# The last four pairs of gate column tiles as seven block products in place of two full ones

## The chip, the cores and the metric

The kernel is one launch on one core of one Trainium2 chip. The metric is the device time of that launch in microseconds (us), taken as the median of several runs; a lower time is better. The engines are named as the profile names them: PE (TensorE, matrix products), PEld (its weight loads), DVE (VectorE), ACT (ScalarE), POOL (GpSimd) and SP (SyncE, which here only issues DMA transfers). Each engine works through its own list of instructions in order and waits on semaphores that other engines and DMA transfers raise.

## The reference, cut to what matters

One decoder layer over 512 tokens of width 1024, all in float32:

```python
proj = h @ w_in                       # 1024 columns in, 4096 out
q, k, v, p, g = split(proj, [512, 1024, 1536, 2048])   # g: 2 x 1024 gate logits
y_attn = moba_attention(q, k, v, rel_bias) @ w_branch_attn
y_pool = multiscale_pool(p, w_pool_group, pool_scale) @ w_branch_pool
gates  = sigmoid(g).reshape(B, S, 2, D)
mixed  = gates[:, :, 0] * y_attn + gates[:, :, 1] * y_pool
h = layer_norm(ALPHA * h + mixed @ w_out, ln1_g, ln1_b)
a, u = split(h @ w_ffn_in, 2)         # 1024 columns in, 2 x 2816 out
f = (gelu(causal_dwconv(a, conv_w, conv_b)) * u) @ w_ffn_out
h = layer_norm(ALPHA * h + f, ln2_g, ln2_b)
```

The change concerns the 2 x 1024 gate columns `g`. Gate tile (0, f) is columns 128 f to 128 f + 127 of the attention gate, (1, f) the same columns of the pool gate; the two with one f are a column pair. The code numbers them `("g", f)` and `("g", 8 + f)`.

## The kernel before, in words

**Precision.** Every large product is made of three products of float32r parts: a tile is split into `hi` (a rounded copy, made on ACT) and `lo` (the rest, made on DVE); `split`, lines 65 to 70. `mm3` (lines 182 to 186) then issues hi·hi, hi·lo and lo·hi.

**Weights.** All weight tiles stand in one list, `chunks`, in the order of their use. `weights(i)` (line 177) fetches ahead up to chunk i + LEAD (3): a transfer issued on SP into one of three `wraw` buffers, then the split into one of RING (5) slots of `whi` and `wlo`.

**Stages.** (1) x is loaded and split into `xT_hi`, `xT_lo` (8 row tiles of 128 x 512, the first named dimension being the contraction). (2) v. (3) Attention in four pairs of heads; `bg()` (line 425) places one column tile of q, k, p or g (24 matmuls of 512 columns, `in_tile`, line 341) between the steps of a head: `scores`, `trans`, `pv`. At head pair 3 the steps and tiles are: scores 6, tile, scores 7, tile, `trans(6)`, tile, `trans(7)`, tile, `pv(3)`. (4) The gate tiles left in `todo` follow without a break: the gates of the first twelve tiles are copied to `gates` by DVE and put through the sigmoid later in place, the last four (NLATE) go through the sigmoid straight into `late`. Meanwhile zT (pool branch) and oT (attention) are split (lines 456 to 459). (5) The branch products `br`, the output projection `wo`, LayerNorm, (6) the channel mixer `fi`, in which ten column pairs (SEVEN, line 40) are made by seven block products, and (7) `fo` with the final LayerNorm.

**Seven block products** (`seven`, lines 693 to 717, for the channel mixer). A column pair has weights A and U of 1024 x 128 each; the 1024 rows are cut in halves k1, k2 and the 512 tokens in halves t1, t2, so that the pair is a 2 x 2 by 2 x 2 block product. Two full tiles need 2 x 24 = 48 matmuls of 512 columns; the seven products need 7 x 12 = 84 of 256 columns. They need, on the activation side, four differences of blocks (T3, nT1, nT2, T4, made by `t_form`, line 663, each 128 x 1024 and each split), and on the weight side, besides A and the second half D of U, two sums: X = U + shifted A, brought by a plain transfer on SP and a second one on POOL that adds as it lands (`fetch_sums`, line 126), and Y, made by two DVE additions (line 144). Three PSUM banks (sa, sb, sc) are taken for a pair; ACT copies three partial sums out (lines 699, 701, 705) and DVE adds three (708, 710, 711). The last product of a pair is held back (`pending`) and issued in the middle of what follows.

**What sets the order.** The program is written in one sequence, and a scheduler that has its own estimate of times places the instructions in the lists of the engines. Tile pools hand out memory; a pool with `reuse_waits="tile"` makes a new tile wait only for the users of the memory that it takes over.

## Time and profile before

| | |
|---|---|
| runs of the kernel before | 651.28, 652.33, 652.54 us, median 652.33 us |
| the profiled execution, its own time | 652.89 us |
| its span, first to last instruction | 651.2 us |
| time outside the span (launch and end) | 652.89 - 651.2 = 1.7 us |
| DVE, ACT, POOL busy | 432.7, 318.1, 106.9 us |
| granted TensorE clock, mean | 0.996 |

How to read the rows in the next part: a timeline row is start, duration (both us), engine, source line, operation, output<-inputs, shapes, count, and in brackets the idle time of that engine ahead of it and what ended it. Rows of groups give busy time and the mean duration of one in ns. A matmul's duration reaches into the next ones; the distance between the starts of two matmuls is what one costs while PE is full. A row with x4 covers four instructions from the start of the first to the end of the last.

### The profile page before, as it was taken

What the parts mean: (1) busy time and instruction counts of PE and PEld (TensorE: products, weight loads), DVE (VectorE), ACT (ScalarE), POOL (GpSimd) and SP (SyncE); (2) the same over time, 40 slices, a digit from 0 to 9 for tenths busy, and PEclk for the clock granted to TensorE, in tenths of its full rate; (3) what the DMA queues carried; (4) which work ended last, traced back from release to release, by engine and by line L of the source; (5) the groups of instructions that cost most, each with busy time, mean ns of one, the idle gap of its engine ahead of it and who ended that gap; (6) DMA issues with size and microseconds to landing.
All of it is one profiled execution on the core that took longest, in us unless ns stands there. A gap on an engine that the chain in (4) does not pass through costs nothing.

```text
span 651.2 us, 8945 instructions
## 1 busy us (share of the span) xinstructions
PE 639.8 (98%) x3442; PEld 548.0 (84%) x3442; DVE 432.7 (66%) x638; ACT 318.1 (49%) x455; POOL 106.9 (16%) x149
## 2 busy tenths in 40 slices
PE   9999999999999999999999999999999999999994
PEld 6888787878788888889999999989898888888884
DVE  6456665564632576299677766776866859798596
ACT  6547556675522333225544544445455337555352
POOL 1605261211000123300010000101000202123302
PEclk9999999999999999999999999999999999999998
DMA  9633222222222237404066665556335895899905
GB/s 324 229 124 104 82 81 82 67 67 94 72 94 100 90 98 285 135 1 161 2 164 171 167 158 160 153 156 165 101 98 162 289 254 131 215 200 201 261 3 129
DMA packets 30363, 91.63 MB, mean 141 GB/s; under 512 B 3560, under 2 KB 3816, under 8 KB 30064
## 3 DMA queue, kind: packets, MB, share of 16 engines
q1 hardware_dynamic: 21744, 65.86, 30.3%
q0 software_dynamic: 8000, 24.14, 18.4%
q10 hardware_dynamic: 576, 1.05, 0.4%
q8 instruction: 27, 0.44, 0.3%
q14 instruction: 16, 0.13, 0.1%
HBM read 87.87 MB, written 3.17 MB: 140 GB/s over the span
## 4 chain that ended last, share of the span: by engine, by line
PE 91%; DVE 3%; DMA 2%; ACT 1%; POOL 1%; issue 1%; DVEq 0%; ACTq 0%; POOLq 0%
PE fi L184 7%; PE fi L186 7%; PE fi L185 7%; PE g L184 5%; PE g L186 4%; PE g L185 4%; PE v L285 3%; PE sa L186 3%; PE sa L184 3%; PE sa L185 3%; PE wo L186 2%; PE br L186 2%; PE wo L185 2%; PE br L185 2%; PE wo L184 2%; PE br L184 2%
## 5 line engine op out<-in xcount | busy, mean ns | idle before, releaser
L70 DVE TENSOR_TENSOR wlo<-wraw,whi 128x1024 fp32r<-128x1024 f32 (+1 forms) x115 | 141.4, 1232 | 69.9 <-ACT whi L69 68.6
L69 ACT ACTIVATE whi<-wraw 128x1024 fp32r<-128x1024 f32 (+1 forms) x114 | 114.6, 1009 | 129.7 <-PE g L185 23.7
L186 PE MATMUL fi<-hT_hi,wlo 128*128 128x512 f32 (+1 forms) x232 | 81.8, 353 | 0.0
L185 PE MATMUL fi<-hT_lo,whi 128*128 128x512 f32 (+1 forms) x232 | 81.8, 353 | 0.0
L184 PE MATMUL fi<-hT_hi,whi 128*128 128x512 f32 (+1 forms) x232 | 81.5, 354 | 0.0
L184 PE MATMUL g<-xT_hi,whi 128*128 128x512 f32 x128 | 50.3, 393 | 0.0
L186 PE MATMUL g<-xT_hi,wlo 128*128 128x512 f32 x128 | 49.9, 390 | 0.0
L185 PE MATMUL g<-xT_lo,whi 128*128 128x512 f32 x128 | 49.9, 390 | 0.0
L186 PEld LDWEIGHTS fi<-hT_hi,wlo 128*128 128x128 f32 x232 | 43.9, 189 | 5.8
L185 PEld LDWEIGHTS fi<-hT_lo,whi 128*128 128x128 f32 x232 | 43.9, 189 | 5.6
L184 PEld LDWEIGHTS fi<-hT_hi,whi 128*128 128x128 f32 x232 | 43.6, 189 | 5.4
L132 POOL DMA_DIRECT2D xraw<-in_w_fi x10 | 12.2, 1220 | 176.2 <-DMA xraw<-in_w_fi 91.9
L69 ACT ACTIVATE whi<-tw 128x1024 fp32r<-128x1024 f32 (+1 forms) x30 | 29.3, 982 | 21.7 <-DMA tw<-in_w_fo 8.5
L70 DVE TENSOR_TENSOR wlo<-tw,whi 128x1024 fp32r<-128x1024 f32 (+1 forms) x30 | 33.3, 1126 | 7.5 <-ACT whi L69 7.5
L186 PEld LDWEIGHTS g<-xT_hi,wlo 128*128 128x128 f32 x128 | 24.0, 188 | 5.1
L184 PEld LDWEIGHTS g<-xT_hi,whi 128*128 128x128 f32 x128 | 24.0, 188 | 5.0 <-issue 0.2
L185 PEld LDWEIGHTS g<-xT_lo,whi 128*128 128x128 f32 x128 | 24.0, 188 | 4.9
L390 POOL TENSOR_SCALAR pp<-pp,rs 128x128 f32<-128x128 f32 (+3 forms) x32 | 21.7, 695 | 37.5 <-PE g L186 18.4
L482 POOL TENSOR_TENSOR mt<-m,m 128x512 f32<-128x512 f32 x8 | 11.1, 1393 | 96.0 <-DVE m L479 79.3
L172 POOL DMA_DIRECT2D tw<-in_w_fo x18 | 15.6, 897 | 60.6 <-DVE wlo L70 60.6
L184 PE MATMUL wo<-whi,mx_hi 128*128 128x512 f32 x64 | 25.0, 391 | 0.0
L186 PE MATMUL wo<-whi,mx_lo 128*128 128x512 f32 x64 | 24.9, 390 | 0.0
(250 smaller groups left out, 1665.0 us busy)
## 6 DMA issues: line engine op xcount, KB each, us to landing
wraw<-in_w_fi SPq DMA_DIRECT2D x34, 512.0 KB, 4.3
wraw<-in_w_c SPq DMA_DIRECT2D x28, 512.0 KB, 3.4
tw<-in_w_fo POOLq DMA_DIRECT2D x20, 512.0 KB, 8.0
xraw<-in_w_fi SPq DMA_DIRECT2D x10, 512.0 KB, 4.4
xraw<-in_w_fi POOLq DMA_DIRECT2D x10, 512.0 KB, 5.8
wraw<-in_w_fo SPq DMA_DIRECT2D x10, 512.0 KB, 5.8
tw<-in_w_fo SPq DMA_DIRECT2D x10, 512.0 KB, 6.4
wraw<-in_w_br SPq DMA_DIRECT2D x8, 512.0 KB, 3.3
```

The costliest lines, as they stand in the source:

```text
L69: nc.scalar.activation(hi, src, AF.Copy)
L70: nc.vector.tensor_tensor(lo, src, hi.bitcast(F32), op=ALU.subtract)
L132: nc.gpsimd.dma_start(v, bass.AP(tensor=a.tensor, offset=a.offset, ap=[[pst, pn], [u.offset + S - a.offset, 2], [est, S]]), accum_op=ALU.add)
L172: nc.gpsimd.dma_start(raw, half(then[1:], sl), accum_op=ALU.add)
L184: nc.tensor.matmul(out_, wh, ah, start=start, stop=False, **kw)
L185: nc.tensor.matmul(out_, wh, al, start=False, stop=False, **kw)
L186: nc.tensor.matmul(out_, wl, ah, start=False, stop=stop, **kw)
L285: nc.tensor.matmul(bs[j], xs_[j][a], (wh, wl)[b], start=kt == 0 and n == 0, stop=False)
L390: nc.gpsimd.tensor_scalar(pp[:, offs[i]:offs[i] + n], pp[:, offs[i]:offs[i] + n], rs[:, i:i + 1], 1.0, op0=ALU.mult, op1=ALU.mult)
L482: nc.gpsimd.tensor_tensor(mt, m[1], m[0], op=ALU.add)
```

## The change

- The order of the column tiles gets "s" entries: after q, k, p and the gate tiles (0,0), (1,0), (0,1), (1,1) come (0,2), (1,2), (0,3), then the pairs f = 4 to 7 as seven products each, and (1,3) last. `bg()` stops at the first "s" entry, so that (0,3) is the last plain tile before `pv(3)`.
- `seven`, `s_mm`, `fetch_seven`, `fetch_sums` and `t_form` become general: the same code serves gates and channel mixer.
- After `pv(3)` a pool `gx` is opened on the memory of the attention tiles. Four transfers on POOL bring x again as four quarters (`quad0` to `quad3`, each 128 x 4 x 256, 512 KB), two more per pair bring X. Then the four differences are formed and split, then the pairs run.
- A pair's gates leave through ACT: `gates_done` applies the sigmoid to bank sa and to u (with scale -1).
- The splits of zT and oT now stand behind the gate pairs, ahead of `br`.

The core of the diff:

```diff
-    order += spare
+    order += [("g", 2), ("g", 10), ("g", 3)] + [("s", f) for f in range(4, KT)] + [("g", 11)]
...
     def in_tile(n):
         kind, j = order[n]
-        wh, wl = split3(weights(C0 + n), KT)
+        if kind == "s":
+            seven(("g", j), (xT_hi, xT_lo), tg, p1s[j % 2], gus[j % 2],
+                  lambda ba, u, j=j: gates_done(j, ba, u))
+            return
+        wh, wl = split3(weights(at[kind, j]), KT)
...
+    def gates_done(j, ba, u):
+        nc.scalar.activation(new_gate(j), ba, AF.Sigmoid)
+        nc.scalar.activation(new_gate(KT + j), u, AF.Sigmoid, scale=-1.0)
...
-    bg(len(todo))
     attn.close()
+    late = actp.enter_context(tc.tile_pool(name="late", bufs=1, side="right", reuse_waits="tile")).tile(
+        [P, NLATE, S], F32, name="late")
+    gxs = ExitStack()
+    gx = gxs.enter_context(tc.tile_pool(name="gx", bufs=1, reuse_waits="tile"))
...
+    quads = []
+    for k in (k1, k2):
+        for t in (t1, t2):
+            v = gx.tile([P, 4, 256], F32, name=f"quad{len(quads)}")
+            nc.gpsimd.dma_start(v, xT[k.start * P:k.stop * P, t].rearrange("(k p) t -> p k t", p=P))
+            quads.append(v)
+    fetch_sums(sums.pop(0))
+    for n in ("nT1", "T3", "nT2", "T4"):
+        t_form(n, tg, *quads)
+    while todo:
+        in_tile(todo.pop(0))
+    flush()
+    gxs.close()
...
-    while todo:
-        in_tile(todo.pop(0))
```

The general pieces that it calls (the first product to the last, in the order written):

```python
def t_form(n, tt, b11, b12, b21, b22):
    if n in ("nT1", "T3"):
        v, a = {"nT1": (b11, b11), "T3": (b12, b22)}[n]
        nc.vector.tensor_tensor(v, a, b12, op=ALU.subtract)
    else:
        v, a = {"nT2": (b22, b11), "T4": (b21, b22)}[n]
        nc.vector.scalar_tensor_tensor(v, a, -1.0, v, op0=ALU.mult, op1=ALU.subtract)
    split(*tt[n], v)

# seven(key, whole, tt, y, u, done):
s_mm(key, "A", 0, b_(k1, t1), chain, True);   nc.scalar.activation(y, chain, AF.Copy)
s_mm(key, "X", 0, tt["T3"], low, True);       nc.scalar.activation(u[:, t2], low, AF.Copy)
flush()
s_mm(key, "Y", 0, tt["nT2"], chain, False);   nc.scalar.activation(u[:, t1], chain, AF.Copy)
s_mm(key, "A", 1, b_(k2, t1), c11, True)
s_mm(key, "D", 0, tt["T4"], low, False);      nc.vector.tensor_tensor(u[:, t1], u[:, t1], low, op=ALU.add)
s_mm(key, "X", 1, tt["nT1"], chain, False);   nc.vector.tensor_tensor(u[:, t2], u[:, t2], chain, op=ALU.add)
nc.vector.tensor_tensor(ba[:, t1], y, c11, op=ALU.add)
# held back: s_mm(key, "Y", 1, b_(k2, t2), chain, False); done(ba, u)
```

In the program as built, the lists of the engines run as follows from the last softmax on. The index in brackets is the pair, "A0" the first half product with weights A, and so on; the lists are the scheduler's.

```
PE    g(0,3) | pv(3) | A0[4] x12 | X0[4] x1 | A1[4] x12 | Y0[4] x1 | A0[5] x2 | X0[4] x11 | X0[5] x2, A1[5] x2,
      Y0[4] x1, D0[4] x1, Y0[4] x10, A0[5] x10, A1[5] x10, X1[4] x12, X0[5] x6, D0[4] x11, ... (pairs interleaved)
      ... Y0[7] x10 | g(1,3) x23 | X1[7] x12 | g(1,3) x1 | Y1[7] x12 | br(0) ...
ACT   sigmoids | copy oT of pv(3) | copy y of A0[4] | nT1_hi | whi X[4] | whi D[4] | T3_hi | nT2_hi | whi Y[4] |
      whi A[5] | whi X[5] | T4_hi | copies u[4] | ...
DVE   copy of g(0,3) | nT1 | nT1_lo | T3 | first half of Y[4] | nT2 | second half of Y[4] | wlo X[4] | wlo D[4] | T4 |
      T3_lo | nT2_lo | wlo Y[4] | wlo A[5] | wlo X[5] | T4_lo | ...
      ... add u[7] behind X1[7] | wlo br(2) | add y + c11 into bank sa[7] | wlo br(3) | zT_lo x4 | oT_lo x4 | ...
POOL  softmax scaling of head 7 x4 | quad0 | quad1 | quad2 | quad3 | adding transfer X[4] | adding transfer X[5] | ...
SP    X[4] | X[5] (both behind the last scores) | A[5] (behind the second half of Y[4], whose input it overwrites) | ...
```

quad0 waits for the last matmul of scores 7. The matmul X0[4] x1 needs T3_hi and whi X[4]; the first of Y0[4] needs nT2_hi and whi Y[4]; the first of A0[5] needs whi A[5]; the first of X0[4] x11 needs T3_lo; the first of Y1[7] waits for the addition into bank sa[7]. The channel mixer and all that follows keep their lists.

## The prediction, on record before the run

> **What bounds the kernel now.** I read the page first: shares of the engines, then the chain that ended last; then the timeline of PE where the change sits, then the rows that price what is added.

> ```profile
> span 651.2 us, 8945 instructions
> PE 639.8 (98%) x3442; PEld 548.0 (84%) x3442; DVE 432.7 (66%) x638; ACT 318.1 (49%) x455; POOL 106.9 (16%) x149
> PE 91%; DVE 3%; DMA 2%; ACT 1%; POOL 1%; issue 1%; DVEq 0%; ACTq 0%; POOLq 0%
> ```

> PE is busy for 98% of the span and holds 91% of the chain. So a matmul less is time won, and a wait of PE is time lost in full. The stretch with the gate tiles shows no gap at all, while DVE and ACT have half of it free:

> ```profile
> 165.00:185.00 20.00, 20.00 (x89) 16.53 (x89) 10.47 (x14) 8.99 (x14) 0.00 (x0) 1.00 0.29 92
> ```

> (columns: PE, PEld, DVE, ACT, POOL busy us, granted clock, DMA share, GB/s). That is an average over 20 us. The change puts four differences and their splits at one point of it, so the point decides, not the average.

> **What is removed from PE.** Eight gate tiles (192 matmuls of 512 columns) become 336 of 256 columns.

> ```profile
> 164.25 0.50 PE L184 MATMUL g<-xT_hi,whi 128*128 128x512 f32 x1
> ...
> 173.90 0.39 PE L184 MATMUL g<-xT_hi,whi 128*128 128x512 f32 x1
> ...
> 179.34 0.39 PE L184 MATMUL g<-xT_hi,whi 128*128 128x512 f32 x1
> ...
> 349.01 0.28 PE L184 MATMUL sa<-hT_hi,whi 128*128 128x256 f32 x1
> ...
> 350.44 0.28 PE L184 MATMUL sb<-T_hi,whi 128*128 128x256 f32 x1
> ```

> From 173.90 to 179.34 lie 24 matmuls of 512 columns: 5.44 / 24 = 0.2267 us each. From 349.01 to 350.44 lie 12 of 256: 0.12 us each (1.43 / 12). So 192 x 0.2267 = 43.5 us becomes 336 x 0.12 = 40.3 us: **-3.2 us**. Half the columns cost 53% of the time, which is why an eighth less arithmetic (5.4 us) gives only this.

> [...]

> **What is added ahead of the pairs, on the other engines.** The prices:

> ```profile
> L69 ACT ACTIVATE whi<-wraw 128x1024 fp32r<-128x1024 f32 x101 | 106.6, 1058 | 126.0 <-PE g L185 23.7 <-PE sa L185 17.8 <-PE br L185 16.1
> L69 ACT ACTIVATE whi<-wraw 128x512 fp32r<-128x512 f32 x13 | 8.2, 628 | 3.7 <-PE sb L185 1.8 <-PE fi L185 0.9 <-DMA wraw<-in_w_v 0.6
> L699 ACT ACTIVATE y<-sa 128x256 f32<-128x256 f32 x10 | 3.6, 380 | 4.4 <-PE sa L186 4.4
> L70 DVE TENSOR_TENSOR wlo<-xraw,whi 128x1024 fp32r<-128x1024 f32 x10 | 12.2, 1225 | 9.1 <-ACT whi L69 9.0
> L70 DVE TENSOR_TENSOR wlo<-wraw,whi 128x512 fp32r<-128x512 f32 x14 | 9.6, 686 | 0.4 <-ACT whi L69 0.3
> L144 DVE TENSOR_TENSOR wraw<-xraw,wraw 128x512 f32<-128x512 f32 x10 | 6.9, 688 | 7.3 <-DMA xraw<-in_w_fi 4.1 <-DMA wraw<-in_w_fi 3.2
> L667 DVE TENSOR_TENSOR hraw<-hraw 128x1024 f32<-128x1024 f32 x2 | 2.4, 1224 | 0.2
> L670 DVE SCALAR_TENSOR_TENSOR hraw<-hraw x2: 1218/1218/1219, 320.7 to 323.0; 128x1024 f32<-128x1024 f32 x2
> wraw<-in_w_c SPq DMA_DIRECT2D x28, 512.0 KB, 3.4
> ```

> So a split of 128 x 1024 is 1.06 us on ACT and then 1.22 on DVE, a difference 1.22. Where the engines stand in the old run when the last softmax is over:

> ```profile
> 150.18 3.02 POOL L390 TENSOR_SCALAR pp<-pp,rs 128x128 f32<-128x128 f32 x4 [5.99 <-DVE rs L387]
> 158.10 0.42 DVE L408 COPY PT<-tr 128x256 f32<-128x256 f32 x1
> 162.05 0.69 DVE L355 COPY gates<-g 128x512 f32<-128x512 f32 x1 [3.53 <-PE g L186]
> 164.36 0.60 ACT L419 ACTIVATE oT<-ob 128x512 f32<-128x512 f32 x1 [0.96 <-PE ob L417]
> 164.86 2.18 ACT L69 ACTIVATE zT_hi<-zT 128x512 fp32r<-128x512 f32 x4
> 165.58 2.50 DVE L70 TENSOR_TENSOR zT_lo<-zT,zT_hi 128x512 fp32r<-128x512 f32 x4 [1.44 <-ACT zT_hi L69]
> 248.24 2.14 POOL L490 DMA_DIRECT2D xs<-in_x  x4
> DMA to landing us min/median/max: 3.6/5.4/7.2
> L132 POOL DMA_DIRECT2D xraw<-in_w_fi x10 | 12.2, 1220 | 176.2 <-DMA xraw<-in_w_fi 91.9 <-DVE y L625 69.5 <-DVE fT L628 14.8
> xraw<-in_w_fi POOLq DMA_DIRECT2D x10, 512.0 KB, 5.8
> ```

> The quarters of x: scores 7 are long done when POOL finishes head 7 at 153.2, so POOL's own list starts them. No row shows a 128 x 4 x 256 transfer. Four of 512 KB on POOL took 0.54 us of issue each and landed after 3.6 to 7.2 us (xs, whose landing line is the last but two); the one with two pieces per row 1.22 us. That puts the last quarter between 153.2 + 1.6 + 3.6 = 158 and 153.2 + 3.7 + 7.2 = 164, and X[4], issued behind it and landing in 5.8, at 161 to 165. I take the middle: both are there before they are used, so the loads cost nothing. The cover is the chain below.

> Now the chain, on the clock of the old run, whose lists are the same up to pv(3). Instructions of one engine overlap by 0.1 us on ACT and 0.08 on DVE (zT_hi: four of 0.62 in 2.18; zT_lo: four of 0.69 in 2.50).

> DVE forms nT1 only behind the copy of gate (0,3): 162.7 to 163.9. ACT has nT1_hi behind the copy oT and behind the copy y of A0[4]. PE starts A0[4] where the old run starts the tile behind pv(3), at 164.25; its twelfth ends at 164.25 + 11 x 0.12 + 0.28 = 165.85. Copy y ends at 166.23, nT1_hi at 167.2. DVE waits there: nT1_lo ends at 168.4, T3 at 169.6. ACT has used that time for whi X[4] and whi D[4]; T3_hi ends at 170.7. PE stood free since 164.25 + 12 x 0.12 = 165.7: **first wait 5.0 us**, although A1[4] needs none of this: it stands behind X0[4] x1 in PE's list.

> PE then runs 13 matmuls to 172.25. DVE after T3: half of Y[4] to 170.2, nT2 to 171.35, other half to 171.97. ACT: nT2_hi to 172.4, whi Y[4] to 173.4: **second wait 1.15 us**. The transfer A[5] on SP waited for that other half, since it overwrites its input: 171.97 + 3.4 = 175.4, whi A[5] to 176.45, and PE, with one matmul done, has waited since 173.5: **third wait 2.9 us**. Behind it on SP's queue stand X[6] and D[5], wanted pairs later. DVE's queue goes on: wlo X[4], wlo D[4], T4, T3_lo by 176.0, nT2_lo by 177.2, wlo Y[4] by 178.3. PE meets each just after, so no further wait of size; if A[5] came sooner, T3_lo at 176.0 would stop PE in its place, so this wait could shrink by 0.4 only.

> In steady state a pair costs DVE 3 x 1.14 + 0.60 + 2 x 0.60 + three adds near 0.4 = 6.5 us and PE 84 x 0.12 = 10.1, as in the channel mixer, where this loop has no gaps. Copies, sigmoids and extra transfers of the pairs lie beside PE there: nothing. The window's DMA share of 0.29 leaves room.

> At the end: Y1[7] waits for the addition into its bank, and PE's list has only one matmul between X1[7] and Y1[7].

> ```profile
> L710 DVE TENSOR_TENSOR u<-u,sa 128x256 f32<-128x256 f32 x10 | 4.2, 419 | 10.1 <-PE sa L186 10.0
> L711 DVE TENSOR_TENSOR sa<-y,sc 128x256 f32<-128x256 f32 x10 | 4.3, 427 | 0.2
> ```

> After X1[7]: 0.16 until its last result, 0.34 for the add, 1.14 for a wlo between, 0.43 for the addition, less 0.23 of the one matmul: **1.85 us**. The moved splits of zT and oT follow: zT_lo's first is done 1.14 + 0.69 = 1.8 us after that addition, while PE has 12 x 0.12 + 0.23 = 1.7 us: nothing, or 0.1. The rest come every 0.60 us against three matmuls of 0.2267; without the interleaving of four `br` tiles it would cost up to oT_lo's 2.4 us more.

> Waits: 5.0 + 1.15 + 2.9 + 1.85 = 10.9. With -3.2: **+7.7 us**.

> **The clock.** A PE that stands for 5 us may be slowed.

> ```profile
> 5.76 1.06 PE L285 MATMUL v<-whi,xT_lo 128*128 128x512 f32 x2
> 6.61 0.84 PE L285 MATMUL v<-whi,xT_hi 128*128 128x512 f32 x2
> ...
> 641.91 0.28 PE L186 MATMUL fo_cut<-whi,sd_lo 128*128 128x256 f32 x1
> 644.00:646.00 2.00, 0.00 (x0) 0.00 (x0) 1.90 (x6) 0.51 (x1) 0.60 (x1) 0.84 1.00 277
> 646.00:648.00 2.00, 0.00 (x0) 0.00 (x0) 1.06 (x2) 0.00 (x0) 0.12 (x1) 0.50 0.48 180
> ```

> At the end of the old run the last matmul is over at 642.2. The window from 644 to 646 has 0.84: the clock fell to half (1 - 0.84) x 2 / 0.5 = 0.64 us before 646, that is 3.2 us after the last matmul. At half clock a matmul of 512 columns took (6.61 - 5.76) / 2 = 0.425 us, 1.87 times the 0.2267. The first wait is 5.0 us, so the clock falls more likely than not; the slowed 13 matmuls vanish in the second and third wait. After 176.45 the work is dense, and the half clock then lasts for 0 to 6 us (at the start, fast spacing came after some 6 us of work); each us loses 1 - 1/1.87 = 0.46. Ends 0 and 2.8; I take 3.5 us, that is **+1.6**, nearer the middle.

> [...]

> **Sum.** The profiled execution: 652.89 - 3.2 + 10.9 + 1.6 = 662.2 us. The median of the runs is 0.56 below its own profile: **661.6 us**.

> **The rivals.**
> (a) The waits without the clock: 652.33 + 7.7 = 660.0. For it: the fall was seen once, after a longer standstill.
> (b) The loads come late: quarters in 1 KB pieces at twice the landing of xs (14 us) put the last at 171, past T3's 168.4, and delay all behind it by 3: about 664.6. Against it: the xs row with 2 MB in some 9 us.
> (c) The other side: the differences are ready in time and the change does what it says. DVE is idle from 158.5 to 162.05, quarters may land from 158; if T3_hi and T3_lo were done by 165.7, only the -3.2 (and 1.85 at the end) would stay: 649.1 to 651.0. It decides at nT1_hi: that must run before the copy of A0[4]. The list of ACT speaks against it, and lists run in order.
> (d) Only part of it: ACT and DVE run the first chain faster than priced, or the third wait is covered, 653.5 to 657.

> **How the numbers follow.** Forecast 0.48, (a) 0.27, (b) 0.12, (c) 0.05, (d) 0.08. The range 657.5 to 665.5 holds the forecast, (a) and most of (b). What this measurement can tell from no change is 0.2%, 1.3 us: slower 0.93 (all but (c) and a rest), faster 0.05, no difference 0.02.

> **What would show it.** Right: PE idle of about 5 us just behind pv(3) and 12 matmuls of bank sa, ended by T3_hi on ACT; two shorter gaps, ended by whi of Y[4] and of A[5]; one near 1.9 us ahead of the last product, ended by the addition on DVE; a granted clock of 0.5 for some us after the first. Matmuls of 256 columns 0.12 us apart. Wrong: nT1_hi ahead of the copy y, a first gap under 2 us, a gap ended by a quarter's DMA, or gaps within pairs 5 to 7.

## The result, and the profile after

The changed kernel takes 663.24 us (median of 4 runs, 660.69 to 665.01); the kernel before, beside it, 651.94 us (4 runs, 651.28 to 652.54). The ratio is 1.017, with a 95% interval of 1.0150 to 1.0189: slower, by 1.7%. The profiled execution took 662.85 us; the prediction's sum for it was 662.2. Two executions that took 1300.16 us (kernel "three pairs, lists held" below) and 3673.94 us (the kernel before) are in a slower state and count in no median and no ratio here.

Three lines of the page of the changed kernel (shares of the engines, chain of waits by engine) and its row of granted clock:

```profile
span 661.1 us, 9324 instructions
PE 641.0 (97%) x3586; PEld 555.8 (84%) x3586; DVE 452.2 (68%) x669; ACT 332.7 (50%) x479; POOL 115.6 (17%) x157
...
PEclk9999999999799899999999999999999999999998
...
PE 88%; DVE 4%; DMA 3%; POOL 2%; ACT 2%; issue 1%; DVEq 0%; ACTq 0%; SPq 0%; POOLq 0%
```

PE is 641.0 us busy against 639.8 before, although it does an eighth less in the pairs, and the clock row has two dents besides its end, 7 and 8. The span grew by 9.9 us. Where that lies is seen on PE's timeline of the changed kernel:

```profile
161.79 2.38 PE L493 MATMUL ob<-PT,vv 128*64 128x512 f32 x16
...
165.51 0.28 PE L248 MATMUL sag<-xT_hi,wlo 128*128 128x256 f32 x1
170.69 0.58 PE L246 MATMUL sbg<-gT_hi,whi 128*128 128x256 f32 x1 [4.90 <-ACT gT_hi L69]
...
173.63 0.38 PE L246 MATMUL sag<-gnT_hi,whi 128*128 128x256 f32 x1
176.54 0.38 PE L246 MATMUL sag<-xT_hi,whi 128*128 128x256 f32 x1 [2.54 <-ACT whi L69]
...
218.74 0.39 PE L248 MATMUL g<-xT_hi,wlo 128*128 128x512 f32 x1
220.89 0.38 PE L246 MATMUL sag<-xT_hi,whi 128*128 128x256 f32 x1 [1.76 <-DVE sag L206]
...
223.04 0.63 PE L246 MATMUL br<-zT_hi,whi 128*128 128x512 f32 x1
```

The last matmul of A0[4] starts at 165.51, the next matmul at 170.69, ended by T3_hi (`gT_hi`) on ACT; A0[5] waits for its `whi`; Y1[7] waits for the addition of line 206. Start to start these are 5.18, 2.91 and 2.15 us, where full work has 0.12, 0.12 and 0.23. The third row is what is missing: no wait stands ahead of 173.63, the first matmul of Y0[4].

From here on one number is used for every kernel: the time from the start of pv(3) (`ob`) to the start of the first branch product (`br`). No work outside this stretch is changed. It is read from the one profiled execution of each kernel. Here it is 223.04 - 161.79 = 61.25 us. In the kernel before:

```profile
161.94 2.37 PE L417 MATMUL ob<-PT,vv 128*64 128x512 f32 x16
...
213.34 0.39 PE L184 MATMUL br<-zT_hi,whi 128*128 128x512 f32 x1
```

51.40 us. So the stretch became 9.85 us longer, and the rest of the span, 599.8 us before and 599.9 us after, is the same within 0.15. That rest is not always the same: over the profiles of this document it lies between 597.9 and 600.8 us. A part of it is the start of the launch. The full clock comes at 3.90 us in the earliest profile (buffer of its own for D) and at 9.45 us in the latest (four pairs), and pv(3) starts at 160.91 us in the one and at 163.31 us in the other. So a difference of a us or two between medians is read with the stretch beside it.

The chain of the first wait, ACT's timeline of the changed kernel, then DVE's:

```profile
165.82 0.38 ACT L195 ACTIVATE p<-sag 128x256 f32<-128x256 f32 x1 [1.01 <-PE sag L248]
166.10 1.05 ACT L69 ACTIVATE gnT_hi<-quad 128x1024 fp32r<-128x1024 f32 x1
...
169.58 1.06 ACT L69 ACTIVATE gT_hi<-quad 128x1024 fp32r<-128x1024 f32 x1 [0.97 <-DVE quad L175]
...
175.43 1.06 ACT L69 ACTIVATE whi<-wraw 128x1024 fp32r<-128x1024 f32 x1 [2.10 <-DMA wraw<-in_w_c]
```

```profile
161.90 0.69 DVE L420 COPY gates<-g 128x512 f32<-128x512 f32 x1 [4.67 <-PE g L248]
162.51 1.22 DVE L175 TENSOR_TENSOR quad<-quad,quad 128x1024 f32<-128x1024 f32 x1
167.18 1.23 DVE L70 TENSOR_TENSOR gnT_lo<-quad,gnT_hi 128x1024 fp32r<-128x1024 f32 x1 [3.46 <-ACT gnT_hi L69]
168.32 1.22 DVE L175 TENSOR_TENSOR quad<-quad,quad 128x1024 f32<-128x1024 f32 x1
...
218.94 0.42 DVE L205 TENSOR_TENSOR gu<-gu,sag 128x256 f32<-128x256 f32 x1 [4.42 <-PE sag L248]
219.28 1.22 DVE L70 TENSOR_TENSOR wlo<-wraw,whi 128x1024 fp32r<-128x1024 f32 x1
220.41 0.42 DVE L206 TENSOR_TENSOR sag<-p,scg 128x256 f32<-128x256 f32 x1
```

Two engines hold each other up. DVE has nT1 ready at 163.73 and then stands for 3.46 us, because its list wants nT1_lo next and ACT has not made nT1_hi; ACT has not, because its list wants the copy of A0[4] first (`p`, 165.82). T3 comes out at 169.54 and T3_hi at 170.64. No row names a quarter's transfer: nT1 starts right behind the gate copy. At the end a `wlo` of 1.22 us stands between the two additions.

The granted clock, from windows of the changed kernel (columns as in the prediction; the clock is third from the end):

```profile
170.00:172.00 2.00, 1.31 (x6) 1.31 (x7) 2.00 (x4) 1.32 (x2) 0.00 (x0) 0.61 0.00 0
172.00:174.00 2.00, 2.00 (x10) 1.75 (x9) 2.00 (x3) 1.33 (x2) 0.00 (x0) 0.54 0.46 133
174.00:176.00 2.00, 0.01 (x1) 0.00 (x0) 2.00 (x3) 0.57 (x1) 0.00 (x0) 1.00 0.85 285
176.00:178.00 2.00, 1.46 (x9) 1.46 (x10) 2.00 (x2) 2.00 (x3) 0.00 (x0) 0.81 0.65 212
178.00:180.00 2.00, 2.00 (x12) 2.00 (x11) 2.00 (x3) 0.77 (x2) 0.69 (x1) 0.50 0.07 26
180.00:182.00 2.00, 2.00 (x16) 2.00 (x16) 2.00 (x3) 0.21 (x1) 0.50 (x1) 0.83 0.38 32
...
220.50:221.50 1.00, 0.61 (x5) 0.61 (x6) 1.00 (x2) 1.00 (x3) 0.00 (x0) 1.00 0.00 0
221.50:222.50 1.00, 1.00 (x8) 1.00 (x7) 1.00 (x3) 1.00 (x3) 0.00 (x0) 0.56 0.93 238
```

A window of 2 us with clock c was at half for (1 - c) x 4 us: 1.56 + 1.84 = 3.4 us behind the first wait, 0.76 + 2.00 + 0.68 = 3.4 us behind the third, and another such time, from 221.62 to 225.04, begins behind the wait at the end and reaches 2 us into the branch products. At half clock matmuls of 256 columns start 0.213 us apart (12 from 171.07 to 173.63), not 0.12.

The 9.85 us add up: -3.2 for the matmuls, 5.06 + 2.79 + 1.92 for the three gaps beyond full work, 1.1 for A1[4] at half clock (2.56 us, not 1.44), 1.5 for the half clock under dense work from 177.2 (3.4 x (1 - 0.12 / 0.213)), 0.6 for the slowed part of Y1[7]: 9.8.

### The profile page after: what moved, and what is told of

It is laid out like the page before. It is cut to its first block, busy times and chain, and to the rows that moved or that the text cites. A ratio compares the mean times of both kernels' runs of the same rounds, so it can differ in the third digit from the quotient of the medians.

```text
span 661.1 us, 9324 instructions
## 1 busy us (share of the span) xinstructions
PE 641.0 (97%) x3586; PEld 555.8 (84%) x3586; DVE 452.2 (68%) x669; ACT 332.7 (50%) x479; POOL 115.6 (17%) x157
## 3 DMA queue, kind: packets, MB, share of 16 engines
q10 hardware_dynamic: 576, 1.05, 0.4%
HBM read 93.12 MB, written 3.17 MB: 146 GB/s over the span
## 4 chain that ended last, share of the span: by engine, by line
PE 88%; DVE 4%; DMA 3%; POOL 2%; ACT 2%; issue 1%; DVEq 0%; ACTq 0%; SPq 0%; POOLq 0%
PE fi L246 6%; PE fi L248 6%; PE fi L247 6%; PE v L347 3%; PE saf L246 3%; PE saf L248 3%; PE saf L247 3%; PE br L246 2%; PE br L247 2%; PE br L248 2%; PE g L246 2%; PE g L247 2%; PE wo L247 2%; PE wo L248 2%; PE wo L246 2%; PE g L248 2%
## 5 line engine op out<-in xcount | busy, mean ns | idle before, releaser
L70 DVE TENSOR_TENSOR wlo<-wraw,whi 128x1024 fp32r<-128x1024 f32 (+1 forms) x119 | 141.0, 1189 | 59.8 <-ACT whi L69 56.7
L69 ACT ACTIVATE whi<-wraw 128x1024 fp32r<-128x1024 f32 (+1 forms) x118 | 117.2, 996 | 104.1 <-PE saf L247 17.4
L143 POOL DMA_DIRECT2D xrawf<-in_w_fi x10 | 12.2, 1218 | 171.7 <-DVE fT L728 80.4
L69 ACT ACTIVATE whi<-tw 128x1024 fp32r<-128x1024 f32 (+1 forms) x30 | 29.4, 984 | 21.0 <-DMA tw<-in_w_fo 7.1
L70 DVE TENSOR_TENSOR wlo<-tw,whi 128x1024 fp32r<-128x1024 f32 (+1 forms) x30 | 33.3, 1128 | 6.0 <-ACT whi L69 6.0
L246 PE MATMUL g<-xT_hi,whi 128*128 128x512 f32 x64 | 25.3, 396 | 0.0
L724 ACT ACTIVATE y<-y 128x512 f32<-128x512 f32 x22 | 13.8, 627 | 22.8 <-DVE y L723 22.8
L248 PE MATMUL g<-xT_hi,wlo 128*128 128x512 f32 x64 | 25.0, 390 | 0.0
L247 PE MATMUL g<-xT_lo,whi 128*128 128x512 f32 x64 | 24.9, 389 | 0.0
L247 PE MATMUL wo<-wlo,mx_hi 128*128 128x512 f32 x64 | 24.9, 389 | 0.0
L580 POOL TENSOR_TENSOR mt<-m,m 128x512 f32<-128x512 f32 x8 | 12.9, 1618 | 65.2 <-DVE m L577 58.1
L246 PE MATMUL saf<-nT_hi,whi 128*128 128x256 f32 x80 | 22.5, 281 | 0.5 <-ACT y L195 0.5
## 6 DMA issues: line engine op xcount, KB each, us to landing
wraw<-in_w_fi SPq DMA_DIRECT2D x34, 512.0 KB, 3.9
wraw<-in_w_c SPq DMA_DIRECT2D x24, 512.0 KB, 3.4
tw<-in_w_fo POOLq DMA_DIRECT2D x20, 512.0 KB, 7.8
xrawf<-in_w_fi SPq DMA_DIRECT2D x10, 512.0 KB, 5.3
xrawf<-in_w_fi POOLq DMA_DIRECT2D x10, 512.0 KB, 6.0
wraw<-in_w_fo SPq DMA_DIRECT2D x10, 512.0 KB, 5.2
tw<-in_w_fo SPq DMA_DIRECT2D x10, 512.0 KB, 5.9
wraw<-in_w_br SPq DMA_DIRECT2D x8, 512.0 KB, 3.4
```

What stands on the lines that cost most here:

```text
L69: nc.scalar.activation(hi, src, AF.Copy)
L70: nc.vector.tensor_tensor(lo, src, hi.bitcast(F32), op=ALU.subtract)
L143: nc.gpsimd.dma_start(v, bass.AP(tensor=a.tensor, offset=a.offset, ap=[[pst, pn], [u.offset + S - a.offset, 2], [est, S]]), accum_op=ALU.add)
L246: nc.tensor.matmul(out_, wh, ah, start=start, stop=False, **kw)
L247: nc.tensor.matmul(out_, wh, al, start=False, stop=False, **kw)
L248: nc.tensor.matmul(out_, wl, ah, start=False, stop=stop, **kw)
```

## The experiments

Theory A is the prediction's: PE waits because DVE and ACT work through their lists in order, and the differences stand in them behind work that waits for PE. Rivals are named with the runs. The diffs are cut to what an edit does, with small helpers written out in place; on which pair or tile it acts stands as a comment. All runs, with the stretch defined above; each ratio is to runs of the kernel before taken beside it (their medians are 651.4 to 651.9 us):

| kernel | median us | ratio to before, 95% interval | stretch us |
|---|---|---|---|
| before | 651.94 | | 51.40 |
| changed | 663.24 | 1.0170 [1.0150, 1.0189] | 61.25 |
| tile (1,3) first | 662.35 | 1.0164 [1.0143, 1.0186] | 62.08 |
| tile first, two edges | 657.43 | 1.0087 [1.0073, 1.0101] | 55.88 |
| first wait filled | 661.84 | 1.0152 [1.0139, 1.0166] | 61.39 |
| two waits filled | 660.91 | 1.0140 [1.0126, 1.0154] | 60.62 |
| last pair reordered | 660.75 | 1.0140 [1.0126, 1.0153] | 59.49 |
| buffer of its own for D | 663.48 | 1.0181 [1.0169, 1.0194] | 63.45 |
| no differences | 654.58 | 1.0044 [1.0028, 1.0060] | 53.30 |
| three pairs, lists held, last pair reordered | 649.26 | 0.9968 [0.9957, 0.9980] | 49.14 |
| three pairs | 656.70 | 1.0068 [1.0055, 1.0080] | 57.11 |
| three pairs, lists held | 653.33 | 1.0027 [1.0013, 1.0041] | 53.04 |
| four pairs, tile first, lists held | 655.95 | 1.0067 [1.0054, 1.0080] | 53.21 |

### Does a tile of work ahead of the pairs hide the chain?

```diff
-    order += [("g", 2), ("g", 10), ("g", 3)] + [("s", f) for f in range(4, KT)] + [("g", 11)]
+    order += [("g", 2), ("g", 10), ("g", 3), ("g", 11)] + [("s", f) for f in range(4, KT)]
```

> Edit: gate tile (1,3), which runs at the end, runs as the first thing behind pv(3), ahead of the four pairs; nothing else. Theory A (lists that run in order): DVE forms nT1 only behind its copy of the last plain tile, and ACT makes nT1_hi only behind its copy of A0[4]; a tile put ahead of the pairs pushes both copies back by its own 24 x 0.2267 = 5.4 us, so the chain starts 5.4 us later too. The wait ahead of X0[4] stays near 5, the two behind it stay near 1.2 and 2.9 (or hide under a half clock as in the changed kernel), and the last pair now has no tile beside it: about 1.2 us ahead of X1[7], 1.0 ahead of Y1[7], 0.3 in the first branch product. Median 663 to 665, against 663.2 of the changed kernel. Theory B (cover is all that lacks: the chain starts when x's quarters have landed): 5.4 us of work hide the first wait, and the half clock with it: 656 to 659.

Measured: 662.35 us, far from theory B, a little under theory A's range; the stretch is 0.83 longer than in the changed kernel. DVE's timeline of this kernel, and PE's:

```profile
169.58 0.69 DVE L420 COPY gates<-g 128x512 f32<-128x512 f32 x1 [7.28 <-PE g L248]
170.19 1.22 DVE L175 TENSOR_TENSOR quad<-quad,quad 128x1024 f32<-128x1024 f32 x1
```

```profile
176.03 0.58 PE L246 MATMUL sbg<-gT_hi,whi 128*128 128x256 f32 x1 [5.06 <-ACT gT_hi L69]
```

DVE stood idle for 7.28 us with the quarters of x at hand, because its list has the copy of the new tile ahead of nT1, and that copy waits for the tile's last matmul. The cover carried the chain along with it. The granted clock of this kernel is 0.50 from 173.42 to 187.07 us, 13.65 us without a break, which is a part of its longer stretch. The next kernel adds two edges of order and nothing else (`made` keeps the instruction that formed T3 and the one that made T3_hi; `issue_after` places what it encloses behind an instruction in its engine's list):

```diff
-        nc.scalar.activation(y, chain, AF.Copy)
+        with tc.issue_after(made["T3", "hi"].ins):        # for pair 4
+            nc.scalar.activation(y, chain, AF.Copy)
...
-            nc.vector.tensor_copy(new_gate(j), b)
+            with tc.issue_after(made["T3", "v"].ins):     # for tile (1,3)
+                nc.vector.tensor_copy(new_gate(j), b)
```

> Edit: as the kernel with tile (1,3) first, and two edges of order: DVE's copy of that tile stands behind the difference T3, ACT's copy of A0[4] behind T3_hi. Theory A: the chain starts at 162.7 again while PE works through the tile. The wait ahead of X0[4] is gone. What stops PE next is the first of Y0[4], about 3 us, for whi Y[4] near 173.4 (its time is set by DVE and ACT, which are no faster), then 0.9, 0.2 and 0.7 for splits on DVE; the wait for A[5] is gone; at the end about 1.85 ahead of Y1[7] and 0.7 in the first branch product. Sum of waits about 7.3 against the 11 of the changed kernel: 3.7 us less, 659.5; down to 657.5 where the clock does not fall. Theory C (x's quarters come late): a wait ended by a quarter's transfer shows, and the time is above 662.

Measured: 657.43 us, just below the low end of the expectation; the stretch is 6.2 us shorter than without the edges. The low end stood for a clock that does not fall. It fell twice, for 3.41 us each (from 175.57 and from 216.53 us), but the gaps came to about 6 us beyond full work, not 7.3. PE's timeline of this kernel:

```profile
172.23 0.28 PE L254 MATMUL scg<-xT_hi,wlo 128*128 128x256 f32 x1
175.48 0.40 PE L252 MATMUL sag<-gnT_hi,whi 128*128 128x256 f32 x1 [2.97 <-ACT whi L69]
...
215.47 0.39 PE L252 MATMUL sag<-xT_hi,whi 128*128 128x256 f32 x1 [1.87 <-DVE sag L212]
```

The wait ahead of X0[4] is gone, and PE meets the next thing in the lists, whi Y[4], 2.97 us, as expected. The order of the lists is shown as the cause of the first wait.

### What does the half clock cost?

```diff
         s_mm(key, "A", 0, b_(k1, t1), chain, True)
+        fill(20)    # pair 4: 20 matmuls on zeros into a bank that nobody reads
         s_mm(key, "X", 0, tt["T3"], low, True)
```

> Edit: the changed kernel with 20 matmuls of 512 columns on a tile of zeros, into a bank that nobody reads, between A0[4] and X0[4]: about 4.3 to 4.5 us of work in the first wait of about 5. No list of another engine changes. The granted clock should stay 1.0 from 170.4 on. Theory A: the half clock of 170.4 to 173.8 was hidden in the second wait, which comes back with 1.15; the third wait ends at the same time as before, since whi A[5] does not hang on PE; so the time is the same within 0.5 us (662.5 to 663.5). Theory D (the clock is a main part of the loss): 1.5 to 3 us less, 660 to 661.7.

> Edit: as the kernel with the first wait filled, and 9 more such matmuls behind the first of Y0[4], in the third wait (about 2 of its 2.9 us). Theory A: the half clock of 177.25 to 180.66 is gone as well, and this one ran under dense work: 3.4 x (1 - 0.12 / 0.213) = 1.5 us come back; by its lists the wait at the end becomes 0.9 us longer (Y1[7] has no matmul of tile (1,3) between it and X1[7]). 661.5 to 663, and 1.5 less than the kernel with the first wait filled if the wait at the end is left out. If the clock falls all the same at 177.25, the fall does not come from PE's idle time in the window before.

Measured: 661.84 and 660.91 us. By its median the first lies between the two theories: 1.4 us under the changed kernel, where A expected none. The stretch settles it: 61.39 against 61.25, so nothing was gained where the edit is, and the 1.4 us lie outside it (the rest of the span is 597.9 us in this profile, 599.9 in that of the changed kernel). PE's timeline of the kernel with the first wait filled:

```profile
164.82 4.49 PE L173 MATMUL fill<-warm 128*128 128x512 bf16 x20
169.88 0.39 PE L260 MATMUL sbg<-gT_hi,whi 128*128 128x256 f32 x1 [0.57 <-ACT gT_hi L69]
...
172.57 0.38 PE L260 MATMUL sag<-gnT_hi,whi 128*128 128x256 f32 x1 [0.87 <-ACT whi L69]
175.45 0.44 PE L260 MATMUL sag<-xT_hi,whi 128*128 128x256 f32 x1 [2.50 <-ACT whi L69]
```

With the clock kept, the second wait is there: 0.87 idle, 1.15 start to start. The first half clock had only been lying in it. The clock still fell behind the third wait; with that filled too (its windows):

```profile
174.00:178.00 4.00, 3.49 (x26) 2.87 (x25) 4.00 (x4) 3.33 (x4) 0.18 (x1) 1.00 0.61 183
178.00:182.00 4.00, 4.00 (x36) 4.00 (x35) 3.96 (x6) 1.41 (x3) 1.02 (x1) 1.00 0.57 81
```

1.00 throughout, and the stretch is 0.77 shorter, though the wait ahead of Y1[7] grew by 0.77 (2.91, not 2.14, start to start). The first 18 matmuls behind the third wait take 3.76 us with the half clock and 2.22 with the wait filled: the second half clock cost 1.5 us. The median is 0.6 under the range of the expectation.

### The end, and the transfer of A[5]

```diff
         s_mm(key, "Y", 0, tt["nT2"], chain, False)
         s_mm(key, "A", 1, b_(k2, t1), c11, True)       # pair 7: behind Y0[7]
-        s_mm(key, "D", 0, tt["T4"], low, False)
         s_mm(key, "X", 1, tt["nT1"], chain, False)
+        s_mm(key, "D", 0, tt["T4"], low, False)        # pair 7: behind X1[7]
```

> Edit: the changed kernel with the last pair alone in another order: Y0[7], A1[7], X1[7], D0[7], held to it by edges on PE's list; tile (1,3) and D0[7] thus stand between X1[7] and Y1[7]. Theory A: the addition into the bank of pair 7 hides behind that work; the wait of 1.8 ahead of Y1[7] goes, and with it the half clock of 221.6 to 225.0 (1.5 us). By the lists a wait of 0.8 comes up ahead of the last product of pair 6 instead. Sum -1.1 for the waits and about -1.5 for the clock: 660 to 661.3. Rival: the splits of zT and oT, which stand behind, are late next and the first branch products wait in its place: 662.5 to 664.

Measured: 660.75 us, as theory A has it; the stretch is 1.76 shorter. No wait stands ahead of Y1[7], the clock stays at 1.00 there, and the new wait came where it was expected (PE's timeline):

```profile
206.81 0.39 PE L254 MATMUL sag<-xT_hi,whi 128*128 128x256 f32 x1 [0.74 <-DVE sag L210]
```

Next, D of the pairs in a buffer of its own:

```diff
+        elif q == "D" and key[0] == "g":
+            raw = gx.tile([P, S], F32, tag="draw", name=f"draw{key[1]}", bufs=1)
         else:
             raw = raws[key, q] = wp.tile([P, D], F32, tag="wraw", name=f"wraw{i}", bufs=3)[:, :n]
```

> Edit: the changed kernel with D of the four pairs loaded into a buffer of its own, so that A[5] no longer overwrites the input of Y[4] and its transfer need not wait for DVE. Theory A (DVE's and ACT's queue of splits is the bound of the start, SP's transfer only the last in it): the wait of 2.9 for A[5] falls to 0.9, and what was hidden behind it shows: 0.7 for whi X[5], 0.2 for T3_lo, 0.3 for nT2_lo, 1.0 for wlo Y[4]; sum 3.1 in place of 2.9. At the end the same lists give 2.7 in place of 1.8 ahead of Y1[7]. 663 to 665, if the clock falls as before; with short waits in place of the long one the second half clock may be gone, then 662. Rival E (the transfer that waits on SP is the cost): 2 to 4 us less, 659 to 661.

Measured: 663.48 us, and no run under 661.9: the time is in theory A's range, and rival E's is not reached. PE's timeline of this kernel:

```profile
173.44 0.58 PE L249 MATMUL sag<-xT_hi,whi 128*128 128x256 f32 x1 [0.27 <-ACT whi L69]
...
187.51 0.39 PE L251 MATMUL sbg<-gT_hi,wlo 128*128 128x256 f32 x1 [1.26 <-DVE wlo L70]
...
221.94 0.39 PE L249 MATMUL sag<-xT_hi,whi 128*128 128x256 f32 x1 [2.63 <-DVE sag L209]
```

The wait of 2.54 for A[5] is down to 0.27, and at that matmul this kernel is 2.2 us ahead of the changed one. It loses the lead in three places. The half clock lasts 10.24 us here, from 167.74 to 177.98 without a break, and takes about 0.9 us of it. At 187.51 PE waits for a split (`wlo` of D[5]) that stands on DVE behind the first half of Y[6], and DVE stood 4.27 us for the adding transfer of X[6] (DVE's timeline):

```profile
186.16 0.69 DVE L158 TENSOR_TENSOR wraw<-xrawg,wraw 128x512 f32<-128x512 f32 x1 [4.27 <-DMA xrawg<-in_w_c]
```

That transfer took 8.9 us from issue to landing (5.7 in the changed kernel); behind this wait the kernel is 1.0 us late. The end adds 1.2 us (0.75 of it in the wait ahead of Y1[7]), so the stretch is 2.2 us longer.

So theory A has the time, but not for its reason: of the 2.2 us that it expected to show up behind the wait for A[5] (whi X[5], T3_lo, nT2_lo, wlo Y[4]), one wait of 0.15 us is there. That the total came out in its range is luck. What the wait for A[5] costs by itself stays open: taking it away won 2.2 us at the spot, and two other things, a longer half clock and a slow transfer of X[6], took them back.

### What the differences cost in all

```diff
-    tg = {n: tuple(gx.tile([P, 4, 256], F32R, name=f"g{n}_{q}") for q in ("hi", "lo"))
-          for n in ("nT1", "T3", "nT2", "T4")}
+    tg = {n: (xT_hi[:, k, t], xT_lo[:, k, t])
+          for n, k, t in (("nT1", k1, t1), ("T3", k1, t2), ("nT2", k2, t2), ("T4", k2, t1))}
```

and the four loads and the four calls of `t_form` for the gates are left out.

> This kernel leaves out the four differences of x, their splits and the four loads of x's quarters; the seven products read blocks of x in their place. All else stays. Theory A: the first, second and third wait come from the differences, so they go; left are 1.6 ahead of X0[4] for whi X[4], and at the end, where the lists now put tile (1,3) elsewhere, 0.1 ahead of Y1[7] and 1.8 in the first branch product for the splits of zT. Sum 3.5, against -3.2 of the matmuls: the stretch takes about what it takes in the kernel before, 652 to 653.5. Rival: the pairs themselves run slower than 84 x 0.12 or wait within (DVE's load): above 656.

Measured: 654.58 us, 1.1 above the range; the stretch is 7.95 shorter than in the changed kernel and 1.9 longer than in the kernel before, where 0.3 was expected. The large waits of the start are gone; two that were not foreseen are there (DVE's timeline):

```profile
183.26 0.69 DVE L155 TENSOR_TENSOR wraw<-xrawg,wraw 128x512 f32<-128x512 f32 x1 [4.86 <-DMA xrawg<-in_w_c]
```

DVE waited 4.86 us for the transfer of X[6], the one that was late in the kernel with a buffer of its own for D too, and PE for 1.05 and 1.16 us start to start behind it. Its plain transfer was issued at 168.51, once DVE had split X[4], whose buffer it takes. The adding one followed at 173.49, 0.56 us behind the landing of the plain one, and landed at 183.18, after 9.7 us, where the other three of this kernel took 5.5 to 7.5. Why it took so long is open.

### Enough cover, and lists that use it

The version that these runs point to: three pairs, so that two tiles are free for the start and one for the end; the differences and Y ahead of all splits; the copies behind.

```diff
+    order += [("g", 2), ("g", 10), ("g", 3), ("g", 4), ("g", 12)] + [("s", f) for f in range(5, KT)] + [("g", 11)]
...
+    vs = {n: t_form(n, tg, *quads) for n in ("nT1", "T3", "nT2")}      # no split yet
+    weights(at["g", 5, "A"])                                           # X, D, Y of pair 5
+    with behind_of(("g", 5), "v"):                                     # behind the halves of Y[5]
+        vs["T4"] = t_form("T4", tg, *quads)
+    with behind_of("T4", "v"):
+        for n in ("T3", "nT2", "nT1", "T4"):
+            made[n, "hi"] = split(*tg[n], vs[n])
```

Further, the two tiles' copies stand behind the halves of Y[5], the copy of A0[5] behind whi Y[5], and the last pair is in the order shown above.

> Edit: three pairs (5 to 7) as seven products; tiles (0,4) and (1,4) run behind pv(3), ahead of the pairs, tile (1,3) stays at the end. DVE's list is held by edges: nT1, T3, nT2, both halves of Y[5], T4, then the splits; the copies of the two tiles and ACT's copy of A0[5] behind them; the last pair in the order Y0, A1, X1, D0. Theory A: 10.9 us of matmuls cover the chain, the end is covered too; one wait of 0.3 is left, and the clock stays. Three quarters of the saving, 2.4: 650.2, in 649.7 to 651; the kernel before is at 651.8. If a wait above 1 us stays at the start the theory lacks a cost.

Measured: 649.26 us, ratio 0.9968 [0.9957, 0.9980]: faster than the kernel before, by 0.3%. Its windows over 48 us of the stretch, DVE's and ACT's timeline at the start:

```profile
162.00:210.00 48.00, 47.89 (x333) 43.57 (x330) 37.15 (x46) 29.31 (x44) 1.20 (x1) 1.00 0.54 149
```

```profile
162.52 2.47 DVE L180 TENSOR_TENSOR quad<-quad,quad 128x1024 f32<-128x1024 f32 x2
165.03 1.23 DVE L183 SCALAR_TENSOR_TENSOR quad<-quad,quad 128x1024 f32<-128x1024 f32 x1
...
172.04 0.68 DVE L437 COPY gates<-g 128x512 f32<-128x512 f32 x1
```

```profile
165.67 1.05 ACT L69 ACTIVATE gT_hi<-quad 128x1024 fp32r<-128x1024 f32 x1
```

PE is busy for 47.89 of 48 us and the clock is 1.00. T3_hi is done at 166.7, 3.9 us earlier than in the changed kernel, and DVE runs from 162.5 to 172.7 without a pause. The stretch is 2.26 shorter than before: three quarters of 3.2 is 2.4. So a pair is worth 0.75 us. Two of its parts alone, the first without any edge, the second without the other order of the last pair; and four pairs with one tile and held lists:

> Edit: three pairs (5 to 7) as seven products, tiles (0,4) and (1,4) behind pv(3) ahead of them, tile (1,3) at the end; no edge holds any list. Theory A: twice the cover of the kernel with tile (1,3) first, but the copies of both tiles stand ahead of nT1 on DVE and the copy of A0[5] ahead of nT1_hi on ACT again. By the lists the waits are 1.6 (T3_hi), 1.4 (whi Y[5]), 1.1 (T3_lo), 1.0 (whi A[6]), none at the end: 5.1, less 2.4 saved: 2.7 above the kernel before, 654.4, and up to 1.5 more if the clock falls. If the cover alone does it (the order held by edges bought nothing): 650 to 651.

> Edit: the kernel of three pairs with held lists, without the other order of the last pair. Theory A: the start stays covered, the wait ahead of Y1[7] is back, 2.7 by the lists: -2.4 + 0.3 + 2.7 = 0.6 above the kernel before, 652.2; up to 653.5 if the clock falls behind that wait.

> Edit: four pairs, tile (1,3) ahead of them, and DVE's list held as in the kernel of three pairs (differences and Y[4] first, splits behind, the copy of the tile and of A0[4] behind Y[4]). Theory A: one tile covers all but 1.7 us of the start (nT2_lo, wlo Y[4], whi X[5]); at the end 1.5 ahead of X1[7], 1.0 ahead of Y1[7], 0.3 in the first branch product, since no tile is left there. Sum 4.5, less 3.2: 1.3 above the kernel before, 653.0; up to 654.5 if the clock falls once.

Measured: 656.70, 653.33 and 655.95 us. One row of PE's timeline of each:

```profile
177.72 0.38 PE L246 MATMUL sbg<-gT_hi,whi 128*128 128x256 f32 x1 [1.42 <-ACT gT_hi L69]
```

```profile
213.38 0.45 PE L255 MATMUL sag<-xT_hi,whi 128*128 128x256 f32 x1 [2.63 <-DVE sag L215]
```

```profile
212.33 0.38 PE L255 MATMUL sag<-gnT_hi,whi 128*128 128x256 f32 x1 [2.60 <-ACT gu L209]
```

Cover alone leaves T3_hi late after 10.9 us of matmuls, with three more waits behind it and 6.8 us of half clock: 0.8 above the range. Without the reordered last pair one wait of 2.63 is left, and in the profiled execution, 654.73 us, the clock falls behind it. The runs of this kernel spread from 651.54 to 655.46 us; their median is inside the range. With four pairs the start is covered by one tile (one wait of 0.29 left there), and the end is not: X1[7] waits 2.60, not 1.5, for a copy that stands on ACT behind a split that waits for a transfer. Its median is 1.5 us above the range. Its stretch is 1.8 longer than before, its median 4.25 us higher. Of the 2.4 us outside the stretch, 1.4 stand ahead of pv(3), where the full clock came at 9.45 us in this profile and at 7.07 us in that of the kernel before; and the profiled execution of the kernel before, from which its stretch is read, is itself 1.2 us above the median beside these runs. Four pairs with held lists and the other order of the last pair in one kernel were not run.

## Why the prediction was right

- **The sum.** 662.2 foreseen for the profiled execution, 662.85 measured; 661.6 and 663.24 for the median, which lies 0.4 above its profiled execution, not 0.56 below it. In the stretch the waits came out 1.1 smaller than foreseen (9.8, not 10.9) and the clock 1.6 larger (3.2, not 1.6), so the sum is nearer than these two terms; that part is luck.
- **The matmuls, -3.2.** Right. Shown without any wait by the three pairs: -2.26 for -2.4. The 20 bf16 matmuls of 512 columns that fill the first wait start closer than the float32r ones do: 20 of them take 4.49 us and the nine in the third wait 2.12 (two waits filled), so (4.49 - 2.12) / 11 = 0.215 us each, not 0.2267.
- **The loads at nothing.** Right: the last quarter landed at 160.90, and nT1 starts behind the gate copy at 162.51 without a wait for one. Rival (b) is out.
- **First wait 5.0.** Measured 5.06, by the chain foreseen, each step within 0.2 us. The two edges showed that the order of DVE's and ACT's lists makes it.
- **Second wait 1.15.** It was not in the profile (rival and forecast alike counted it); it lay under the slowed A1[4], which cost 1.1. With the clock kept it measured 1.15 start to start, 1.03 beyond full work.
- **Third wait 2.9.** Measured 2.79. But the sentence that this wait could shrink by 0.4 only, since T3_lo would stop PE in its place, is not borne out: with a buffer of its own for D the matmul behind this wait came 2.2 us sooner, and PE did not wait for T3_lo.
- **End 1.85.** Measured 1.92, by the `wlo` between the additions; reordering the last pair took it away. The moved splits of zT and oT cost nothing that shows.
- **No gaps in pairs 5 to 7.** Right in the changed kernel.
- **The clock, +1.6.** This term was too small. The fall behind the first wait came, and its slowed matmuls did vanish in a wait, as said. But the step "after 176.45 the work is dense, and the half clock then lasts for 0 to 6 us" took one fall that goes on; there were two separate ones of 3.4 us, the one behind the first wait and one behind the third, with the full clock between, and a third behind the wait of 1.9 at the end, which the prediction did not count. The first cost 1.1 (in the place of the second wait), the second 1.5, the third 0.6 inside the stretch and an estimated 0.9 behind it (2.0 us of branch products at 0.427 us a matmul, not 0.2267).
- **Not foreseen.** A wait of 0.51 us in the channel mixer at 364.64, whose lists are the same. ACT's copy of an A0 ended it, which stood on ACT behind a split. Five of the twelve profiles of changed kernels have it (0.51 to 0.72 us), a sixth has 0.3 us there (tile first), the others do not; why is open.

Rival (a), the waits without the clock at 660.0, is what the kernel with two waits filled comes to: 660.91, with a wait at the end that is 0.77 longer and one half clock left behind it. Rival (c), the differences ready in time, needed what the prediction named: nT1_hi ahead of the copy of A0[4]. The kernel of three pairs with held lists does that, with two tiles as cover, and is faster than before; with four pairs and one tile the stretch stays 1.8 longer.

## What to carry to other kernels

Work that is put in as cover for a chain helped here only where no instruction of the chain stood behind the cover's own evacuation (the copy of its result) in an engine's list; look at the list, and put the first links of the chain (here the differences) ahead of the copies and splits that wait for PE. A saving of a few us spread over a stage is easily less than the one-time cost of its set-up at a point where PE has nothing else; give up a part of the saving (here one pair of four) to keep plain work for both ends of the stage.

## What the runs showed of the hardware that was not expected

| kernel | piece, us | PE idle in it, us | clock in the next piece |
|---|---|---|---|
| changed, ahead of Y1[7] | 218.21 to 221.62 | 1.76 | 0.50 |
| four pairs, tile first, lists held | 207.42 to 210.84 | 1.11 | 1.00 |
| the same | 210.84 to 214.25 | 1.73 | 1.00 |
| three pairs | 176.27 to 179.69 | 1.58 | 1.00 |
| three pairs | 179.69 to 183.10 | 1.93 | 0.50 |

- An estimate from these rows: a single gap of under 1.7 us keeps the clock if PE works without a pause around it, one of over 3.5 us loses it, since one piece then holds at least 1.76 us of it, and between the two it depends on where the grid lies. At half clock no such bound shows: the piece from 171.15 to 174.57 us with 0.42 us of idle time (buffer for D) was followed by one more at half, the piece from 3.17 to 6.58 us with 0.46 (changed kernel, matmuls of 512 columns 0.40 us apart at its end) by the full clock.
- The fall came late: in the changed kernel the gap ends at 220.89, and the clock is still 1.00 then; it is 0.5 from 221.6 to 225.0, when PE is busy again. So work that is dense paid for the gap before it. By these runs a gap of 2.14 us can already be too long (tile first with two edges, first wait filled), and by the estimate above what counts is the idle time within a piece of 3.41 us.
- Matmuls on zeros kept the clock: 20 of them in a wait of 5 us, 4.49 us long (first wait filled), and the clock stayed at 1.00 behind it until 175.64; in the changed kernel, without them, it is 0.50 from 170.42.
